# Conditioning tiles moved to another buffer ring, a further expert block taken into the loop, and a down projection placed inside the next block's gate and up

## The chip, the cores and the metric

The kernel runs on one core of one Trainium2 chip. The metric is device time in microseconds (us) of one execution. A core has five engines with a queue each: TensorE (PE, with its weight loads as PEld), VectorE (DVE), ScalarE (ACT), GpSimd (POOL) and SyncE (SP). In this kernel SP issues nearly all plain loads and stores, and POOL issues gathers, scatters and broadcasts. Sixteen DMA engines carry all of them.

## The reference

A backbone of two layers works on 512 tokens of width 1024, in float32. Layer 0 (even) has neighbourhood attention beside a short convolution, layer 1 (odd) has Hyena channels beside a conformer convolution. Each layer ends in a mixture of 16 experts with two experts per token. Shift, scale and gate of every part come from a conditioning vector:

```python
sh1, sc1, g1, sh2, sc2, g2 = split(silu(c) @ ada_w[l] + ada_b[l], 6)
u = rmsnorm(x, norm1_g[l]) * (1 + sc1) + sh1
y = odd_mixer(u, ...)                      # layer 1: w_in_odd, then long and short convolutions
x = x + g1 * (y @ w_out[l])
x = x + g2 * hier_moe(rmsnorm(x, norm2_g[l]) * (1 + sc2) + sh2, ...)
# hier_moe: act = silu(t @ w_gate) * (t @ w_up) * weight;  sum over experts of act @ w_down
```

The six conditioning vectors of a layer are three pairs: j=0 is (sh1, sc1), j=1 is (g1, sh2), j=2 is (sc2, g2). For layer 1, pair 0 is needed at the odd stage's start, pairs 1 and 2 only after it.

## The kernel before

**Split weights.** Every large product is made from three matmuls of rounded halves. A weight tile of 512 KB is loaded into a ring of five buffers called raw (L136). `split` (L141) lets ACT round it into a tile whi (L145), and DVE subtracts to make wlo (L146); whi and wlo each have four buffers. `mm3` issues the three matmuls (L159 to L161). A buffer is used again when all readers of its last content are done, so the SP load of a raw tile waits for the readers of the tile that lay there, and everything behind it in SP's queue waits too.

**The odd stage (about 587 to 845 us).** A string, ORDER (L65), sets the sequence of its pieces: v, p and x are projections of the three Hyena operands by column quarter, c the conformer's quarters, A and B the two long convolutions (as matrix products, L621 and L807), L a layer norm. Between the letters, tN takes N steps of a generator, `self.ada1` (L1111), that works pairs 1 and 2 of the conditioning through `ada_sums` (L230). For each pair it loads 16 tiles of ada_w, 512 KB each, into the same ring raw (`self.spare` is empty by then). DVE multiplies each tile by its column of silu(c) and adds it into adaacc (L246, L248). PE sums adaacc over the partitions (L254) into a PSUM bank, and `ada_done` adds the bias adab, which POOL has loaded at the generator's start (L235). For pair 2, `gain_rows` (L302) loads gainr through POOL (L305) and DVE multiplies it in (L307). The result goes to memory through SP (L268), and POOL reads it back spread over 128 partitions as gb (`bcast`, L323).

**After the odd stage** `mid` (L935) projects with w_out, adds the residual with the gate gb (L999, L1000), normalises with hm (L982), routes the tokens, and runs the expert blocks.

**Expert blocks.** Each expert takes up to 128 tokens as one block. POOL gathers the rows (L1307), PE turns them (L1318) and ACT and DVE split them into xt (L1321, L1324). `gate_up` (L1355) takes four weight tiles u=0 to 3: three are split, and the fourth goes unsplit through L1364 where the block is listed in FU. ACT and DVE make the activation (L1371, L1372), PE turns it (L1375), and L1378 and L1379 split it into at. `down` (L1383) takes two further tiles, and DVE scales the result into eo (L1396). POOL then adds it to memory by an indirect scatter (L1397); each scatter waits for the one before it. In the loop, the down of block b-1 is issued after the gate and up of block b (`late`).

**The further block.** If an expert has more than 128 tokens, the surplus makes a 17th block. In this run layer 1 has one such block and layer 0 none: there are 17 scatters to out and 16 to xd. The kernel before handles it in `extra_blocks` (L1117), under a run-time condition behind the whole loop: turn, six loads, gate and up, and down.

The order of instructions on each engine is set by a scheduler when the program is built, from the program order, buffers and dependencies.

## Time and profile before

| what | value |
|---|---|
| three runs of before | 1123.34, 1126.87, 1130.07 us (median 1126.87) |
| profiled execution | 1123.78 us |
| its span in the trace | 1121.7 us |
| mean granted TensorE clock | 0.944 |
| PE busy | 1023.0 us (91%) |
| DVE busy | 774.0 us (69%) |
| ACT busy | 497.9 us (44%) |
| POOL busy | 230.4 us (21%) |
| DMA | 240.78 MB, mean 215 GB/s |

The span is what the trace covers; the execution's own time is 2.1 us longer. Busy times are sums over instructions of one engine. A wait is idle time of an engine put down to whatever released it last, and the chain of waits follows the last instruction back through whatever released each step. Times in the rows are microseconds from the span's start.

### The profile page before, as it was taken

What the parts mean: (1) busy time and instruction counts of PE and PEld (TensorE: products, weight loads), DVE (VectorE), ACT (ScalarE), POOL (GpSimd) and SP (SyncE); (2) the same over time, 40 slices, a digit from 0 to 9 for tenths busy, and PEclk for the clock granted to TensorE, in tenths of its full rate; (3) what the DMA queues carried; (4) which work ended last, traced back from release to release, by engine and by line L of the source; (5) the groups of instructions that cost most, each with busy time, mean ns of one, the idle gap of its engine ahead of it and who ended that gap; (6) DMA issues with size and microseconds to landing.
All of it is one profiled execution on the core that took longest, in us unless ns stands there. A gap on an engine that the chain in (4) does not pass through costs nothing.

```text
span 1121.7 us, 14655 instructions
## 1 busy us (share of the span) xinstructions
PE 1023.0 (91%) x5118; PEld 755.2 (67%) x5118; DVE 774.0 (69%) x1255; ACT 497.9 (44%) x787; POOL 230.4 (21%) x244
## 2 busy tenths in 40 slices
PE   6999999999999599999987889899899859999994
PEld 2786787556787477777756667576477747777663
DVE  3462335587658798897967677757754577998883
ACT  3352223356434476577625323221253236766652
POOL 2031304011053223354221000000002121333311
PEclk8999999998999599999988899899989778999998
DMA  8825563686364479999825657634418786799893
GB/s 342 319 68 166 164 198 128 245 267 220 121 222 177 153 228 349 307 317 299 270 61 205 224 148 232 192 94 142 140 56 268 258 269 211 242 307 322 283 291 79
DMA packets 75374, 240.78 MB, mean 215 GB/s; under 512 B 15887, under 2 KB 17706, under 8 KB 75296
## 3 DMA queue, kind: packets, MB, share of 16 engines
q1 hardware_dynamic: 59840, 209.82, 55.0%
q0 software_dynamic: 15456, 29.98, 10.6%
q8 instruction: 42, 0.69, 0.3%
q14 instruction: 36, 0.29, 0.1%
HBM read 227.40 MB, written 25.72 MB: 226 GB/s over the span
## 4 chain that ended last, share of the span: by engine, by line
PE 65%; DMA 17%; DVE 8%; issue 5%; ACT 3%; POOL 1%; SPq 0%; POOLq 0%; DVEq 0%; ACTq 0%
PE mm L159 13%; PE mm L160 13%; PE mm L161 12%; DMA out<-eo,gi 6%; PE mm L225 3%; PE mm L1364 3%; PE sc L621 3%; PE mm L807 3%; DMA raw<-in_w_in_odd 2%; PE mm L580 2%; DVE wlo L146 2%; PE mm L621 2%; PE tr L1318 2%; DMA raw<-in_moe 2%; PE tr L569 2%
## 5 line engine op out<-in xcount | busy, mean ns | idle before, releaser
L146 DVE TENSOR_TENSOR wlo<-raw,whi 128x1024 fp32r<-128x1024 f32 x199 | 242.8, 1231 | 93.9 <-ACT whi L145 93.2
L145 ACT CAST whi<-raw 128x1024 fp32r<-128x1024 f32 x199 | 206.6, 1051 | 159.8 <-DMA raw<-in_w_in_odd 59.9
L159 PE MATMUL mm<-whi,xt 128*128 128x512 f32 x208 | 87.0, 418 | 2.4 <-ACT whi L145 2.4
L160 PE MATMUL mm<-wlo,xt 128*128 128x512 f32 x208 | 85.6, 412 | 3.3 <-DVE wlo L146 3.0
L161 PE MATMUL mm<-whi,xt 128*128 128x512 f32 x208 | 83.9, 403 | 0.0
L159 PE MATMUL mm<-u,whi 128*128 128x512 f32 x160 | 65.8, 414 | 5.9 <-ACT whi L145 5.3
L1307 POOL DMA_INDIRECT xe<-hd,gi x34 | 44.9, 1320 | 108.5 <-PE tr L1318 81.9
L161 PE MATMUL mm<-u,wlo 128*128 128x512 f32 x160 | 64.4, 404 | 0.3 <-DVE wlo L146 0.2
L160 PE MATMUL mm<-u,whi 128*128 128x512 f32 x160 | 64.4, 404 | 0.0
L1318 PE MATMUL tr<-ident,xe 128*128 128x128 f32 x264 | 41.6, 285 | 18.3 <-DMA xe<-hd,gi 16.0
L159 PE MATMUL mm<-whi,at 128*128 128x512 f32 x132 | 54.6, 448 | 1.0 <-ACT at L1378 0.9
L1396 DVE SCALAR_TENSOR_TENSOR eo<-mm,sw,gb 128x512 f32<-128x512 f32 x66 | 47.6, 744 | 10.6 <-PE mm L161 10.4
L160 PE MATMUL mm<-wlo,at 128*128 128x512 f32 x132 | 53.1, 417 | 0.0
L1397 POOL DMA_INDIRECT out<-eo,gi x17 | 33.2, 1953 | 96.1 <-DVE eo L1396 36.1
L1321 ACT CAST xt<-tr 128x512 fp32r<-128x512 f32 x66 | 32.4, 496 | 43.6 <-PE tr L1318 43.3
L161 PE MATMUL mm<-whi,at 128*128 128x512 f32 x132 | 51.0, 407 | 0.6 <-DVE at L1379 0.6
L1318 PEld LDWEIGHTS tr<-ident,xe 128*128 128x128 f32 x264 | 33.4, 148 | 26.3 <-issue 18.4
L160 PEld LDWEIGHTS mm<-wlo,xt 128*128 128x128 f32 x208 | 40.5, 195 | 14.7 <-DVE wlo L146 6.3
L159 PEld LDWEIGHTS mm<-whi,xt 128*128 128x128 f32 x208 | 40.3, 194 | 11.5 <-ACT whi L145 3.3
L1397 POOL DMA_INDIRECT xd<-eo,gi x16 | 33.3, 2079 | 71.7 <-DVE eo L1396 44.7
L1324 DVE TENSOR_TENSOR xt<-tr,xt 128x512 fp32r<-128x512 f32 x66 | 37.4, 570 | 14.8 <-ACT xt L1321 10.6
L743 POOL MEMSET pad<- 128x1 f32 x12 | 1.2, 100 | 225.5 <-DVE x L750 158.0
(402 smaller groups left out, 2439.0 us busy)
## 6 DMA issues: line engine op xcount, KB each, us to landing
raw<-in_moe SPq DMA_DIRECT2D x143, 512.0 KB
raw<-in_ada_w SPq DMA_DIRECT2D x64, 512.0 KB
mr<-in_moe SPq DMA_DIRECT2D x47, 512.0 KB
raw<-in_w_in_odd SPq DMA_DIRECT2D x20, 512.0 KB
bias<-in_ada_w SPq DMA_DIRECT2D x16, 512.0 KB
raw<-in_w_out SPq DMA_DIRECT2D x16, 512.0 KB
raw<-in_w_qkv SPq DMA_DIRECT2D x12, 512.0 KB
raw<-in_w_gch SPq DMA_DIRECT2D x12, 512.0 KB
```

Source lines behind the costliest of these rows:

```text
L145: nc.scalar.copy(hi, raw3)
L146: (lo_engine or nc.vector).tensor_tensor(lo, raw3, hi, op=ALU.subtract)
L159: nc.tensor.matmul(ps, lh, rh, start=first, stop=False)
L160: nc.tensor.matmul(ps, lh, rl, start=False, stop=False)
L161: nc.tensor.matmul(ps, ll, rh, start=False, stop=last)
L225: nc.tensor.matmul(ps[32 * g:32 * g + 32, :], self.cT[:, k, :], raws[g // 2][:, (g % 2) * 512:(g % 2) * 512 + 512], start=(k == 0), stop=( ...
L621: nc.tensor.matmul(ps[:, g * 256:g * 256 + 256], D[:, mat, :], s[:, r, :], start=(n == 0), stop=(n == 1))
L1307: self.fetched = self.nc.gpsimd.indirect_dma_start(out=xe, out_offset=None, in_=self.hd[l][:, :], in_offset=bass.IndirectOffsetOnAxis(ap=g ...
L1318: nc.tensor.transpose(pt[:, k * 128:k * 128 + 128], xe[:, (4 * h + k) * 128:(4 * h + k) * 128 + 128], self.ident)
L1324: nc.vector.tensor_tensor(xt[:, 1, 4 * h:4 * h + n, :].rearrange("p a b -> p (a b)"), pt[:, 0:n * 128], hi, op=ALU.subtract)
L1396: nc.vector.scalar_tensor_tensor(o[:, sl], ps, wt, g2b[:, sl], op0=ALU.mult, op1=ALU.mult)
L1397: nc.gpsimd.indirect_dma_start(out=self.dst[l][:, :], out_offset=bass.IndirectOffsetOnAxis(ap=di, axis=0), in_=o, in_offset=None, bounds_c ...
```

## The change

Three things are changed.

1. In `ada_sums`, the 32 ada_w tiles of layer 1's pairs 1 and 2 no longer go into ring raw. They take turns in the rings of whi and wlo, under the name adaw. The generator has two more stops per pair, ORDER takes two steps at c0, c2, c1 and c3 and none at A0 and B0 in exchange, and the bias load adab stands at the end of a pair and no longer at its start.
2. NXS says for each layer whether the further block is part of the loop. For layer 1 it is, without a condition: the loop has 17 blocks, SP reads the expert's number from xi (L1091 of the changed kernel), and the loads use the layer's usual rings. For layer 0 the condition stays.
3. In the last block of both layers, the down of the block before is issued between the second and third weight tile of gate and up (`mid=late`).

```diff
--- before.py
+++ after.py
@@ -32,7 +32,7 @@
 WA = [1, 1, 1, 0]
 CX = [2, 4]
 WE = [1, 0, 0, 0]
-XS = 1
+NXS = (0, 1)
 LF = 2
 RG = [2, 3, 4]
 KS = 4
@@ -58,11 +58,11 @@
 SB = 2
 QC = 0
 FE = 0
-FU = [[0, 1, 3, 4, 5, 6, 7, 8, 9, 10, 11, 12, 13, 14, 15], [1, 2, 3, 5, 6, 8, 9, 10, 11, 12, 13, 15]]
+FU = [[0, 1, 3, 4, 5, 6, 7, 8, 9, 10, 11, 12, 13, 14, 15], [1, 2, 3, 5, 6, 8, 9, 10, 11, 12, 13, 15, 16]]
 PM = 1
 PJ = 2
 PU = [[], []]
-ORDER = 'p1 t1 v1 t1 v0 t1 p0 t1 c0 t1 A0 t1 v3 t1 v2 t1 p2 t1 c2 t1 p3 t1 c1 t1 A1 x0 t1 c3 t1 x1 t1 B0 t1 x2 L0 x3 B1 t9'
+ORDER = 'p1 t1 v1 t1 v0 t1 p0 t1 c0 t2 A0 v3 t1 v2 t1 p2 t1 c2 t2 p3 t1 c1 t2 A1 x0 t1 c3 t2 x1 t1 B0 x2 L0 x3 B1 t9'
 TWO_PI = (6.28125, 0.0019350051879882812, float(2.0 * math.pi - 6.28125 - 0.0019350051879882812))
 P_, Q_ = (0, 1, 2, 3), (4, 5, 6, 7)
 NP1, NP2, NQ2, NQ3 = 8, 9, 10, 11
@@ -231,15 +231,14 @@
 
         nc, A = self.nc, self.A
         b = A["ada_b"]
-        bias = self.wk.tile([128, 512], F32, tag="t2", name="adab")
-        nc.gpsimd.dma_start(bias, bass.AP(tensor=b.tensor, offset=b.offset + l * 6144 + j * 2048,
-                                          ap=[[512, 4], [0, 32], [1, 512]]))
         for h in range(2):
             acc = self.ep2.tile([128, 1024], F32, tag="adaacc", name="adaacc", bufs=1)
             c0 = j * 2048 + h * 1024
             for k in range(8):
-                raw = self.spare.pop(0) if self.spare else self.rawp.tile([128, 1024], F32, tag="raw", name="raw")
-                if self.spare:
+                if l and j:
+                    raw = self.wp.tile([128, 1024], F32, tag=("whi", "wlo")[k % 2], name="adaw")
+                else:
+                    raw = self.spare.pop(0)
                     self.spare.append(raw)
                 nc.sync.dma_start(raw, A["ada_w"][l, k * 128:k * 128 + 128, c0:c0 + 1024])
                 if k == 0:
@@ -253,7 +252,13 @@
             for g in (2 * h, 2 * h + 1):
                 nc.tensor.matmul(ps[32 * g:32 * g + 32, :], self.onec.to_broadcast([128, 32]), acc[:, (g % 2) * 512:(g % 2) * 512 + 512],
                                  start=True, stop=True)
+            if not h:
+                yield
+        bias = self.wk.tile([128, 512], F32, tag="t2", name="adab")
+        nc.gpsimd.dma_start(bias, bass.AP(tensor=b.tensor, offset=b.offset + l * 6144 + j * 2048,
+                                          ap=[[512, 4], [0, 32], [1, 512]]))
         self.ada_done(l, j, ps, bias)
+        yield
 
     def ada_done(self, l, j, ps, bias):
         nc, A = self.nc, self.A
@@ -1077,19 +1082,23 @@
             xt = self.turn(rows[0], 0 in FU[l], m2)
             R["more"]()
             R["weights"]()
-        for b in range(16):
+        nb = 16 + NXS[l]
+        for b in range(nb):
             with self.tc.issue_after(self.routed.ins), self.tc.issue_after(self.last.ins):
                 self.tick(FILT[1] if b >= FB else FC)
-            load = self.ffn_weights(l, b, after=self.fetch0 if b >= EH[l] else None)
+            e = b
+            if b == 16:
+                e = nc.values_load(R["xi"][0:1, 1:2], engines=[mybir.EngineType.SP], min_val=0, max_val=15)
+            load = self.ffn_weights(l, e, after=self.fetch0 if b >= EH[l] else None, ring=b == 16)
             fetch(b + 1 + LA[l])
-            if b < 15:
+            if b < nb - 1:
                 nxt = self.turn(rows[b + 1], b + 1 in FU[l], m2)
             with self.tc.issue_after(self.routed.ins) if b == 0 else ExitStack(), self.tc.issue_after(self.lastT.ins):
-                part, xt = self.gate_up(m2, xt, load, b in FU[l], [i - 6 * b for i in PU[l]]), nxt
+                part, xt = self.gate_up(m2, xt, load, b in FU[l], [i - 6 * b for i in PU[l]], late if b == nb - 1 else None), nxt
             if b == 0:
                 with self.tc.issue_after(self.routed.ins):
                     self.extra_list(mp, R)
-            if late:
+            if late and b < nb - 1:
                 late()
             def late(a=(part, load, g2b, sel("gi", b), sel("wt", b), [i - 6 * b for i in PU[l]], [i - 2 * b for i in DE[l]])):
                 self.down(l, m2, *a)
@@ -1122,11 +1131,11 @@
 
         nc, nx, xi = self.nc, R["nx"], R["xi"]
         SP, DVE = mybir.EngineType.SP, mybir.EngineType.DVE
-        with self.tc.If(nx > 0):
-            if XS:
+        if not NXS[l]:
+            with self.tc.If(nx > 0):
                 xt = self.turn(xe, True, m2)
-            e = nc.values_load(xi[0:1, 1:2], engines=[SP], min_val=0, max_val=15)
-            self.ffn(l, m2, xt, g2b, R["gi"][:, 16:17], R["wt"][:, 16:17], e)
+                e = nc.values_load(xi[0:1, 1:2], engines=[SP], min_val=0, max_val=15)
+                self.ffn(l, m2, xt, g2b, R["gi"][:, 16:17], R["wt"][:, 16:17], e)
         with self.tc.If(nx > 1):
             with self.tc.For_i(1, nx, 1) as i:
                 e = nc.values_load(xi[0:1, bass.ds(i + 1, 1)], engines=[SP], min_val=0, max_val=15)
@@ -1325,11 +1334,11 @@
                                     op=ALU.subtract)
         return xt, xf
 
-    def ffn_weights(self, l, e, early=False, after=None):
+    def ffn_weights(self, l, e, early=False, after=None, ring=False):
 
         nc, A = self.nc, self.A
         src = A["moe"][l][e] if isinstance(e, int) else A["moe"][l][bass.ds(e, 1)].rearrange("o i p c -> (o i) p c")
-        where = "rrrrrr" if not isinstance(e, int) else PF[l][e] if e < len(PF[l]) else RING[l]
+        where = RING[l] if ring else "rrrrrr" if not isinstance(e, int) else PF[l][e] if e < len(PF[l]) else RING[l]
         for i in range(6):
             if where[i] == "b" and not early:
                 yield self.early[l, e, i]
@@ -1352,12 +1361,14 @@
         load = self.ffn_weights(l, e)
         return self.down(l, m2, self.gate_up(m2, xt, load, True), load, g2b, di, wt)
 
-    def gate_up(self, m2, xt, load, full, pool=()):
+    def gate_up(self, m2, xt, load, full, pool=(), mid=None):
 
         nc = self.nc
         xt, xf = xt
         ps = self.mmt()
         for u in range(4):
+            if u == 2 and mid:
+                mid()
             raw = next(load).rearrange("p (k c) -> p k c", k=2)
             if full and u == 3:
                 for k in range(2):
```

**SP at the start of the odd stage**, behind the loads xr of the layer's input. raw and adaw are the loaded tiles, in_w_in_odd the odd stage's projection weights, and in_ada_w the conditioning weights. Before:

```order
L136 DMA raw_5655<-in_w_in_odd 128x1024
L244 DMA raw_5697<-in_ada_w 128x1024
L244 DMA raw_5700<-in_ada_w 128x1024
L136 DMA raw_5703<-in_w_in_odd 128x1024
L244 DMA raw_5742<-in_ada_w 128x1024
L244 DMA raw_5745<-in_ada_w 128x1024
L136 DMA raw_5748<-in_w_in_odd 128x1024
L244 DMA raw_5787<-in_ada_w 128x1024
L244 DMA raw_5790<-in_ada_w 128x1024
L136 DMA raw_5793<-in_w_in_odd 128x1024
L244 DMA raw_5832<-in_ada_w 128x1024
```

After the change:

```order
L136 DMA raw_5655<-in_w_in_odd 128x1024
L136 DMA raw_5701<-in_w_in_odd 128x1024
L136 DMA raw_5746<-in_w_in_odd 128x1024
L136 DMA raw_5791<-in_w_in_odd 128x1024
L136 DMA raw_5837<-in_w_in_odd 128x1024
L243 DMA adaw_5695<-in_ada_w 128x1024
L243 DMA adaw_5698<-in_ada_w 128x1024
L243 DMA adaw_5740<-in_ada_w 128x1024
L243 DMA adaw_5743<-in_ada_w 128x1024
L136 DMA raw_5869<-in_w_in_odd 128x1024
L136 DMA raw_5901<-in_cfx 128x1024
```

Projection loads and conditioning loads alternated in one ring; now five projection loads stand in front, and the conditioning loads have buffers of other rings.

**POOL behind the odd stage**, from the layer norm's lnr on. gb is the gate read back from memory, gainr the norm gain, wr and cst the router's constants. Before:

```order
L192 TENSOR_TENSOR lnr_6961<-lnr_6959,mhalf_94 128x4
L323 DMA gb_7141<-ada11_79 128x1024 x2
L305 DMA gainr_7119<-in_norm2_g 64x1x512
L953 DMA wr_7147<-in_wr 128x160
L955 DMA cst_7149<-in_br 128x20
```

After the change:

```order
L192 TENSOR_TENSOR lnr_6953<-lnr_6951,mhalf_94 128x4
L328 DMA gb_7141<-ada11_79 128x1024 x2
L258 DMA adab_7115<-in_ada_b 128x1x512
L310 DMA gainr_7119<-in_norm2_g 64x1x512
L958 DMA wr_7147<-in_wr 128x160
```

The bias load of pair 2 now stands between the gate's two reads and the load of gainr; before, it was issued during the odd stage (row of L235 at 689.0 us in the trace). On DVE the addition `adar<-mm,adab` moved with it, to directly ahead of `adar<-adar,gainr`.

**DVE at the end of layer 1's experts.** xt are the split token rows, wlo a split weight tile, act and at the activation, eo the scaled result (L1324, L146, L1372, L1379 and L1396 before; L1333, L146, L1383, L1390 and L1407 after). Before:

```order
L1396 SCALAR_TENSOR_TENSOR eo_9416<-mm_9417,sw_7663,gb_7144 128x512
L1396 SCALAR_TENSOR_TENSOR eo_9416<-mm_9425,sw_7663,gb_7144 128x512
L1293 TENSOR_LOAD xi_7848
L1125 COMPARE_AND_BRANCH
L1324 TENSOR_TENSOR xt_9437<-tr_9439,xt_9437 128x512
L1324 TENSOR_TENSOR xt_9437<-tr_9446,xt_9437 128x256
L146 TENSOR_TENSOR wlo_9468<-raw_9465,whi_9467 128x1024
L146 TENSOR_TENSOR wlo_9480<-raw_9477,whi_9479 128x1024
L146 TENSOR_TENSOR wlo_9492<-raw_9489,whi_9491 128x1024
L146 TENSOR_TENSOR wlo_9517<-raw_9514,whi_9516 128x1024
L146 TENSOR_TENSOR wlo_9523<-raw_9520,whi_9522 128x1024
L1372 TENSOR_TENSOR act_9505<-act_9505,mm_9464 128x256
```

After the change:

```order
L146 TENSOR_TENSOR wlo_9459<-raw_9456,whi_9458 128x1024
L146 TENSOR_TENSOR wlo_9465<-raw_9462,whi_9464 128x1024
L1390 TENSOR_TENSOR at_9386<-tr_9383,at_9386 128x256
L146 TENSOR_TENSOR wlo_9491<-raw_9488,whi_9490 128x1024
L1407 SCALAR_TENSOR_TENSOR eo_9468<-mm_9469,sw_7663,gb_7144 128x512
L146 TENSOR_TENSOR wlo_9516<-raw_9513,whi_9515 128x1024
L1407 SCALAR_TENSOR_TENSOR eo_9468<-mm_9477,sw_7663,gb_7144 128x512
L146 TENSOR_TENSOR wlo_9522<-raw_9519,whi_9521 128x1024
L1383 TENSOR_TENSOR act_9504<-act_9504,mm_9431 128x256
L1390 TENSOR_TENSOR at_9510<-tr_9507,at_9510 128x256
L1407 SCALAR_TENSOR_TENSOR eo_9525<-mm_9526,sw_7663,gb_7144 128x512
L1407 SCALAR_TENSOR_TENSOR eo_9525<-mm_9534,sw_7663,gb_7144 128x512
```

The further block's work stood in a row of its own behind the 16th block's last eo (eo_9416); now its five wlo stand around the 16th block's two eo (eo_9468), and the branch is gone.

## Rows read from the trace of the kernel before

**Rows 1.** The page, busy time of the engines and the chain that ended last, whole span.

```profile
PE 1023.0 (91%) x5118; PEld 755.2 (67%) x5118; DVE 774.0 (69%) x1255; ACT 497.9 (44%) x787; POOL 230.4 (21%) x244
...
PE 65%; DMA 17%; DVE 8%; issue 5%; ACT 3%; POOL 1%; SPq 0%; POOLq 0%; DVEq 0%; ACTq 0%
```

**Rows 2.** Windows in the odd stage: us, PE, PEld, DVE, ACT, POOL busy, clock, DMA, GB/s.

```profile
600.00:840.00 240.00, 220.54 (x1098) 155.81 (x1099) 173.55 (x197) 69.03 (x95) 5.28 (x30) 0.94 0.49 151
...
620.00:630.00 10.00, 4.97 (x14) 3.25 (x13) 5.52 (x6) 2.87 (x4) 0.00 (x0) 0.72 0.82 238
...
700.00:710.00 10.00, 4.88 (x13) 3.77 (x14) 6.01 (x6) 2.97 (x5) 0.00 (x0) 0.66 0.77 220
...
790.00:800.00 10.00, 7.97 (x27) 5.68 (x27) 6.26 (x9) 2.57 (x5) 0.00 (x0) 0.83 0.59 165
```

**Rows 3.** Waits in 587 to 845 us: engine line, releaser, total, times, longest.

```profile
ACT whi L145 <- DMA raw<-in_w_in_odd: 59.9, 13, 10.6
```

**Rows 4.** The chain of waits through the odd stage: start us, us, what.

```profile
615.21 1.20 DVE adaacc L248
616.43 8.96 DMA raw<-in_w_in_odd
625.41 1.05 ACT whi L145
...
695.06 8.13 DMA raw<-in_w_in_odd
...
712.12 3.46 PE sc L621 x16
...
772.06 3.44 DMA raw<-in_w_in_odd
```

**Rows 5.** The timeline at the second stall: start us, us, engine, instruction, idle before.

```profile
704.80 1.12 PE L760 MATMUL tr<-ident,x 128*128 128x128 f32 x4 [5.19 <-ACT ur L761]
...
706.23 5.46 PE L621 MATMUL sc<-ur,D 128*128 128x256 f32 x16 [0.32 <-ACT ur L761]
```

**Rows 6.** The page, one of the costliest groups (count, busy, mean ns, idle before).

```profile
L146 DVE TENSOR_TENSOR wlo<-raw,whi 128x1024 fp32r<-128x1024 f32 x199 | 242.8, 1231 | 93.9 <-ACT whi L145 93.2
```

**Rows 7.** The chain at the end of layer 0's experts.

```profile
570.12 1.42 DVE eo L1396 x2
...
571.81 6.31 DMA xd<-eo,gi
...
578.85 6.50 DMA xd<-eo,gi
```

**Rows 8.** POOL's timeline there: start us, us, engine, instruction, idle before.

```profile
562.39 2.41 POOL L1397 DMA_INDIRECT xd<-eo,gi  x1 [7.31 <-DVE eo L1396]
```

**Rows 9.** The chain after the odd stage.

```profile
845.04 12.12 DMA gainr<-in_norm_g
...
868.33 0.69 DVE hm L982
```

**Rows 10.** A window of 10 us behind that chain.

```profile
870.00:880.00 10.00, 7.89 (x27) 5.87 (x28) 6.95 (x8) 4.40 (x8) 2.18 (x1) 0.66 1.02 394
```

**Rows 11.** The timeline of layer 1's end, DVE, ACT and PE.

```profile
1095.36 0.75 DVE L1396 SCALAR_TENSOR_TENSOR eo<-mm,sw,gb 128x512 f32<-128x512 f32 x1 [0.18 <-PE mm L161]
...
1096.80 3.90 ACT L145 CAST whi<-raw 128x1024 fp32r<-128x1024 f32 x4
...
1106.72 0.38 ACT L1371 ACTIVATE act<-mm 128x256 f32<-128x256 f32 x1 [2.59 <-PE mm L1364]
...
1111.62 0.75 DVE L1396 SCALAR_TENSOR_TENSOR eo<-mm,sw,gb 128x512 f32<-128x512 f32 x1 [0.18 <-PE mm L161]
```

**Rows 12.** The chain of layer 1's scatters.

```profile
1093.08 6.92 DMA out<-eo,gi
...
1100.76 6.86 DMA out<-eo,gi
...
1112.65 1.55 POOL out L1397
```

## Prediction

> **What bounds the kernel now.** I read the page first. PE is busy for 1023.0 of 1121.7 us, DVE for 774.0, and of the chain that ended last 65% is PE and 17% DMA [rows 1]. So most of the time is matmul, and what a change of order can win lies where PE stands still or runs slow. The windows show where that is in the odd stage: over 600 to 840 us PE is busy for 220.54 of 240 us, so 19.5 us are idle, and three windows of 10 us hold most of it, with 4.97, 4.88 and 7.97 us busy and granted clocks of 0.72, 0.66 and 0.83 [rows 2]. The waits then name the releaser: ACT's rounding whi waits 59.9 us in 13 waits for projection loads, 10.6 us the longest [rows 3]. Most of that is covered, since PE still has split tiles to work on; it is uncovered in the three windows.
>
> The chain tells why these loads come late. At 615.21 DVE multiplies a conditioning tile (adaacc). Only when it ends is its raw buffer free, and only then, at 616.43, does SP issue the next projection load; it takes 8.96 us, and whi starts at 625.41. The same happens at 695.06 (8.13 us) and, shorter, at 772.06 (3.44 us) [rows 4]. So a projection tile, needed at once, waits in one ring behind a conditioning tile that nothing needs before 845 us. The second stall also shows the clock: PE is idle for 5.19 us behind a small ACT copy that stands behind the late whi, and its next 16 matmuls take 5.46 us [rows 5], where 16 of the same line take 3.46 us at 712.12 [rows 4].
>
> **The odd stage's ring (part 1 of the change).** Added and removed work is nil: 32 loads, 32 DVE multiplies and four PE sums per pair stay. What moves is who waits. The projection loads now have ring raw to themselves, five stand first in SP's queue, and their buffers come free when the wlo of an earlier tile is done.
>
> - First stall: 10 less 4.97 is 5.0 us idle. A mean clock of 0.72 means that 56% of the window, 5.6 us, was granted half speed (1.2 instead of 2.4 GHz), which costs from nothing (all of it in the idle time) to 2.8 us; I take 1.5. Sum 6.5.
> - Second: 5.19 idle and 5.46 less 3.46 for the slow matmuls, 7.2.
> - Third: 10 less 7.97 is 2.0 idle; 0.83 means 3.4 us at half speed, up to 1.7 lost; I take 1. Sum 3.
>
> Together 16.7, taken as 17 us. The most that could go: the three windows hold 12.2 of the 19.5 us idle; all of these, half of the other 7.3 (whose releasers are several), and 2.8, 2.0 and 1.7 for the clock make 22.3. The least is nothing, and less than nothing is the last rival.
>
> A page of the Trainium skill says the time of matmuls should not be read by busy share: "Perfetto Trace Analysis", section Identifying the Most-Contended Engine, holds that matmul busy time is a poor measure of the headroom. The trace agrees with it here, for the 16 matmuls count as busy at 5.46 us as they do at 3.46. By busy share alone the three stalls would give 12.2 us, and the whole sum would be 4.5 us smaller.
>
> What is late next is the new wait. A conditioning tile now holds a buffer of whi or wlo, four each, and two steps apart the split that wants that buffer waits for the tile's load and its multiply. The load takes 3.44 to 8.96 us by the rows of loads [rows 4], the multiply 1.2, so a tile stays for 5 to 10 us. The stage's 240 us hold 16 pairs of tiles, 15 us for each pair, and a buffer returns after four allocations, about two such times. So I cost it at nothing.
>
> **The bias load (also part 1).** adab of pair 2 is 256 KB and stood in the middle of the odd stage. It now stands on POOL between the two reads of gb and gainr. Queued behind it are gainr, DVE's multiply, the store of the pair, its reading back, and hm. In the trace gainr lands 12.12 us after its issue at 845.04, and hm starts at 868.33 [rows 9]. Behind it PE is uncovered: 7.89 us busy at a clock of 0.66 [rows 10], so what is added here is added to the end. The 12.12 us carry the 1024 KB of gb and the 128 KB of gainr; 256 KB at that rate are 2.7 us, and one more DVE addition of about 0.69 us (hm's row) stands in the chain. Bounds: 0, if the bias lands beside the others, and 3.4. I take 3, by the rate's row.
>
> By "DMA: Bandwidth & Descriptors" of the Trainium skill, section Queues, rings and completion order, each DMA engine takes the queues in turn, packet by packet, so POOL's queue would get an even share beside SP's. At half of the 394 GB/s of the later window that would be an estimate of 1.3 us, and the sum would be 1.4 lower; no run here shows the packets in turn, and the 12.12 us speak for a smaller share.
>
> **Layer 0's last block (part 3).** In the chain, block 14's eo ends at 571.5 and its scatter runs from 571.81 for 6.31, then block 15's from 578.85 for 6.50; the next layer's loads wait for that one [rows 7]. Block 14's down now comes ahead of the second half of block 15's gate and up. The scatter before began at 562.39 [rows 8]; at 6.4 us and 0.6 of gap, block 14's could begin at 569.4 instead of 571.81, so 2.4 us are the most. Block 15's own eo must then be earlier too, which its later half does not promise, so 0 is the least; I take the middle, 1.2.
>
> **Layer 1's end (parts 2 and 3).** Block 15's eo ends at 1096.1. The further block then runs alone: four roundings in 3.90 us from 1096.80, the activation at 1106.72, its last eo at 1111.62 [rows 11], 16.3 us behind block 15's. In the loop its turn, splits and matmuls lie beside block 15's. What then binds is the chain of scatters: 1093.08 and 6.92, 1100.76 and 6.86, so the last could begin at 1107.6 and 0.7, 1108.3, instead of 1112.65 [rows 12]: at most 4.4 us earlier. Block 15's down now comes behind half of the further block's gate and up, but its scatter had to wait until 1100.76 anyhow, 4.7 us behind its eo; that is the cover, and if it does not do, the gain shrinks by as much. I take 4, least 0. SP reads xi once more ahead of later expert loads; the nearest row is the gap of 0.76 us between two scatters, where POOL reads it, so 0 to 0.8, and I take 0, since 17 loaded tiles of other buffers lie ahead. The work of the further block is the same, because this layer does have one.
>
> **Sum.** 17 and 1.2 and 4 gained, 3 lost: 19.2 us. Against the profiled execution's 1123.8 us (span 1121.7) that is 1104.6; this execution is 3.1 us below the median of the three runs, 1126.87, and against the median the sum gives 1107.7, which I forecast.
>
> **Rivals.**
>
> *The odd stage gives most of it back.* SP is still one queue in order. Where a conditioning load waits for a whi buffer that PE has not left, the projection load behind it waits as before, only for PE instead of DVE. For it: in the changed order conditioning loads still stand ahead of projection loads after the first five. Against it: the five prefetched tiles. If only 5 of the 17 us remain, the sum is 7.2 and the time 1119.7. Chance 0.13.
>
> *The end gains nothing, and only the ring pays.* Block 15's scatter may begin late, for its down now stands behind more splits on DVE (1.23 us each [rows 6]). With neither end paying the sum is 14 and the time 1112.9. Chance 0.14.
>
> *Slower, through the split buffers.* If a conditioning tile stays longer than those two step times, some 30 us, or if DVE comes to its multiply late because it stands behind a wlo whose tile has not landed, each of the 16 pairs holds back a split by a multiply and a subtraction, 1.2 and 1.23 us [rows 4, 6], together 2.4. Sixteen times that is 39 us, and with the other terms the time is 1126.9 less 19.2 and 39, 1147. It decides from 1.2 us per pair on, where the whole gain is gone. For it: DVE is in order and busy for 173.55 of 240 us [rows 2]. Against it: a stay of 5 to 10 us. Chance 0.08.
>
> **How the numbers follow.** The forecast has the remaining 0.65. About 0.5%, 5.6 us, is what a measurement of this kernel can tell from no change, so faster means below 1121.2. The forecast and the second rival lie below it (0.79); the first lies at it, and I give half of it to each side; the slower rival counts as slower but for 0.01. So faster 0.85, same 0.08, slower 0.07. Best bounds (22.3, 2.4, 4.4 and no bias) sum to 29.1, so 1098; the first rival with 2 us more is 1122. Those are the range.
>
> **What would show it.** Right: ACT's wait for projection loads falls from 59.9 us to below 20, the three windows are filled at full clock, the odd stage ends 15 to 19 us earlier, gainr lands about 3 us later behind gb, and the last scatter follows the one before it within 1 us. Wrong: whi waits for PE or DVE in the odd stage (a split buffer), SP's queue stands at adaw, or PE's idle time comes back among the experts, where the DMAs or the scatters would then be what binds.

## The result and the profile after

The changed kernel takes 1111.32 us in the median of four runs (1110.59 to 1112.4), before took 1126.39 us beside it (1123.34 to 1130.07). The ratio is 0.9871, its 95% interval 0.9834 to 0.9908: 15 us faster, where 19.2 had been forecast, and inside the range of 1098 to 1122. The profiled execution took 1110.59 us, its span is 1108.8 us, 12.9 less than the span of before. The page, busy time of the engines:

```profile
PE 1017.9 (92%) x5118; PEld 749.5 (68%) x5118; DVE 774.1 (70%) x1255; ACT 497.9 (45%) x787; POOL 233.7 (21%) x244
```

The instructions are as many as in [rows 1]. PE's busy time is 5.1 us lower for the same 5118 instructions, DVE's is the same, so some 8 of the 12.9 us are idle time of PE. The table follows the gain along the two profiled executions. Each row is a stretch between two events that both traces have.

| stretch | before | after | gained | forecast |
|---|---|---|---|---|
| start to the 13th scatter to xd (identical work) | 547.24 | 545.08 | 2.16 | none |
| to the last scatter to xd (layer 0's end) | 31.61 | 30.95 | 0.66 | 1.2 |
| loads of layer 1's input (585.37; 582.50) to the gate's read gb (843.86; 830.45) | 258.49 | 247.95 | 10.5 | 17 |
| gb to the first hm (867.72; 857.33) | 23.86 | 26.88 | -3.0 | -3 |
| hm to the last scatter (1112.65; 1099.50) | 244.93 | 242.17 | 2.8 | 4 |

The first row is no effect of the change: PE, DVE, ACT and POOL run the same instructions in the same order up to there, and the traces of the experiments below reach that scatter between 543.9 us (e11) and 547.9 us (e12; e9, which has a smaller ring, is left out). So of the 12.9 us of span about 11 are the change's.

**The odd stage**, in five pieces that hold the same work in both kernels, but for up to four matmuls at each cut. Columns: us, busy us (x instructions) of PE, PEld, DVE, ACT and POOL, granted clock, DMA share, GB/s. Before:

```profile
585.40:600.00 14.60, 8.50 (x36) 6.13 (x34) 7.55 (x18) 8.12 (x21) 2.51 (x4) 0.85 0.92 338
600.00:640.00 40.00, 34.91 (x145) 27.57 (x146) 30.26 (x35) 15.01 (x19) 2.08 (x10) 0.87 0.63 199
640.00:700.00 60.00, 56.48 (x297) 42.12 (x295) 45.73 (x51) 17.83 (x25) 1.65 (x11) 1.00 0.59 176
700.00:790.00 90.00, 83.70 (x432) 55.55 (x432) 63.96 (x71) 20.11 (x28) 0.26 (x4) 0.96 0.49 147
790.00:843.90 53.90, 49.36 (x243) 33.80 (x244) 35.04 (x46) 19.98 (x29) 1.33 (x6) 0.91 0.30 95
sum 258.50, PE 232.94 PEld 165.17 DVE 182.54 ACT 81.05 POOL 7.83; mean PE 46.59 PEld 33.03 DVE 36.51 ACT 16.21 POOL 1.57
```

After the change:

```profile
582.50:597.00 14.50, 11.59 (x40) 8.14 (x38) 7.96 (x18) 9.42 (x22) 2.51 (x4) 0.74 0.95 367
597.00:636.00 39.00, 35.14 (x145) 28.13 (x146) 30.62 (x34) 13.39 (x18) 1.37 (x9) 0.87 0.63 226
636.00:696.00 60.00, 56.71 (x297) 40.39 (x296) 43.90 (x50) 19.75 (x28) 1.40 (x11) 1.00 0.53 164
696.00:778.00 82.00, 80.31 (x428) 53.52 (x426) 64.60 (x71) 19.41 (x29) 0.25 (x4) 1.00 0.53 165
778.00:830.40 52.40, 48.76 (x246) 32.97 (x247) 35.59 (x45) 17.97 (x26) 1.29 (x5) 0.93 0.25 76
sum 247.90, PE 232.51 PEld 163.16 DVE 182.67 ACT 79.95 POOL 6.82; mean PE 46.50 PEld 32.63 DVE 36.53 ACT 15.99 POOL 1.36
```

PE's busy time is 232.94 and 232.51 us, so over the whole stage nearly all of the 10.5 us are idle time: 25.6 before, 15.4 now. The fourth piece is 8 us shorter (90 and 82). Its idle time fell by 4.6 us and its busy time by 3.4, with four matmuls fewer and a granted clock of 1.00 instead of 0.96. It holds the second stall of [rows 2]; the third lies across its end at 790 us. The first two pieces together, with the first stall, gave 1.1 us. The stalls are better told apart between events of PE that both traces have:

| stretch of the odd stage | before | after | gained | forecast |
|---|---|---|---|---|
| loads of the input to the transposition of v ahead of the second stall (698.57; 694.40) | 113.20 | 111.90 | 1.3 | 6.5, first stall |
| to the third product sc<-Di,T (782.18; 770.61) | 83.61 | 76.21 | 7.4 | 7.2, second stall |
| to the next matmuls of wide (798.97; 785.54) | 16.79 | 14.93 | 1.9 | 3, third stall |
| to the gate's read gb | 44.89 | 44.91 | 0.0 | none |

Three further traces below have the same ring and the same late bias load: e1, e5 (the changed kernel again) and e7. Against the same trace of before they gained 3.2, 1.7 and 1.5 us in the first row, 7.4 in the second in all three, and 0.0, -0.1 and 2.4 in the third. A second trace with the old ring (e2) has 113.4, 83.0 and 19.3 us there. So the second row is firm, while the others differ among traces of one ring by as much as they gained.

Which waits of PE those were, by the view of waits (engine line, releaser, total, times, longest). Before, 600 to 840 us:

```profile
PE mm L159 <- ACT whi L145: 5.3, 2, 5.0
PE tr L760 <- ACT ur L761: 5.2, 1, 5.2
PE sc L621 <- ACT b L624: 3.2, 1, 3.2
```

After, 597 to 827 us:

```profile
PE mm L253 <- DVE adaacc L247: 2.8, 1, 2.8
PE mm L161 <- DVE wlo L146: 2.5, 2, 2.1
...
PE tr L351 <- DVE u L359: 1.6, 1, 1.6
```

The three entries of before, 13.7 us, are gone from the list; in their place stand two waits that hang on the conditioning tiles, 2.8 and 2.5 us, and one on the stage's input. The wait of 2.8 us is the third stall under another name: it lies in the same product, between its 8th and 9th matmul. Before (PE), and after (PE, then ACT):

```profile
792.03 7.00 PE L621 MATMUL sc<-ur,D 128*128 128x256 f32 x24 [3.22 <-ACT b L624]
```

```profile
779.13 1.05 PE L253 MATMUL mm<-adaacc,onec 128*32 128x512 f32 x4 [2.80 <-DVE adaacc L247]
780.11 5.50 PE L626 MATMUL sc<-ur,D 128*128 128x256 f32 x24
```

```profile
775.86 1.04 ACT L145 CAST whi<-raw 128x1024 fp32r<-128x1024 f32 x1 [4.22 <-DMA adaw<-in_ada_w]
...
777.96 0.56 ACT L629 COPY b<-sc 128x512 f32<-128x512 f32 x1
```

PE's sum of adaacc stood ahead of this product before (785.84) and now stands inside it, and it waits for the last multiply, which ends at 779.07. The copy b, which PE waited for before, would have held it until 778.52 anyhow, again behind a late whi, and that whi now waits for the landing of a conditioning tile.

ACT's own waits changed their releaser [rows 3]:

```profile
ACT whi L145 <- DVE adaacc L247: 28.8, 4, 11.7
...
ACT whi L145 <- PE mm L160: 19.7, 7, 4.6
```

No load of a projection weight holds ACT any more in this trace. A multiply (adaacc) holds it instead, 28.8 us in four waits, because the split tile's buffer lies behind a conditioning tile. How that comes about at the stage's start is seen on three engines. DVE, in order:

```profile
610.54 0.76 DVE L245 TENSOR_SCALAR adaacc<-adaw,cT 128x1024 f32<-128x1024 f32 x1
...
611.81 1.28 DVE L247 SCALAR_TENSOR_TENSOR adaacc<-adaw,cT,adaacc 128x1024 f32<-128x1024 f32 x1
...
613.73 1.28 DVE L247 SCALAR_TENSOR_TENSOR adaacc<-adaw,cT,adaacc 128x1024 f32<-128x1024 f32 x1
614.92 1.22 DVE L146 TENSOR_TENSOR wlo<-raw,whi 128x1024 fp32r<-128x1024 f32 x1
...
618.79 1.28 DVE L247 SCALAR_TENSOR_TENSOR adaacc<-adaw,cT,adaacc 128x1024 f32<-128x1024 f32 x1 [0.86 <-DMA adaw<-in_ada_w]
```

SP at the same time, and then ACT:

```profile
597.60 0.33 SPq L136 DMA_DIRECT2D raw<-in_cfx  x1
615.03 0.33 SPq L243 DMA_DIRECT2D adaw<-in_ada_w  x1
```

```profile
620.11 1.05 ACT L145 CAST whi<-raw 128x1024 fp32r<-128x1024 f32 x1 [7.73 <-DVE adaacc L247]
```

The first four conditioning tiles were issued at 587 to 592 us, but DVE does not multiply one before 610.54, since in its order the stage's input comes first. The third multiply ends at 615.01, and only then is a buffer free for the fifth tile, whose load SP has held until 615.03 (13.6 us in SP's waits), with everything behind it. That tile's multiply begins at 618.79, and the whi that needs its buffer at 620.11; PE has other tiles by then and waits 0.38 us for the wlo that follows. The wlo at 614.92 stands behind three multiplies; PE waits 2.12 us for it.

**Behind the odd stage**, POOL and DVE (columns: start us, us, engine, instruction, idle before it and its releaser):

```profile
830.45 1.16 POOL L328 DMA_DIRECT2D gb<-ada  x2 [8.76 <-PE mm L161]
832.28 0.72 POOL L258 DMA_DIRECT2D adab<-in_ada_b  x1 [0.67 <-DVE yc L894]
833.00 0.70 POOL L310 DMA_DIRECT2D gainr<-in_norm_g  x1
```

```profile
844.33 0.69 DVE L266 TENSOR_TENSOR adar<-mm,adab 128x512 f32<-128x512 f32 x1 [6.05 <-DMA adab<-in_ada_b]
846.61 0.68 DVE L312 SCALAR_TENSOR_TENSOR adar<-adar,gainr 64x512 f32<-64x512 f32 x1 [1.58 <-DMA gainr<-in_norm_g]
...
857.33 1.29 DVE L987 TENSOR_TENSOR hm<-xr,gb 128x512 f32<-128x512 f32 x2 [4.51 <-DMA gb<-ada]
```

The bias load adab stands between gb and gainr. DVE waits 6.05 us for it. From gb to the gain's multiply it is 16.16 us (830.45 to 846.61); before it was 13.32 (843.86 to 857.18), where gainr alone was waited for [rows 9].

**Layer 0's end** (POOL) and **layer 1's end** (POOL, and the chain of waits there):

```profile
568.28 1.78 POOL L1408 DMA_INDIRECT xd<-eo,gi  x1 [6.78 <-DVE eo L1407]
...
576.03 1.58 POOL L1408 DMA_INDIRECT xd<-eo,gi  x1 [2.57 <-DVE eo L1407]
```

```profile
1092.74 1.55 POOL L1408 DMA_INDIRECT out<-eo,gi  x1 [6.04 <-DVE wlo L146]
1099.50 1.55 POOL L1408 DMA_INDIRECT out<-eo,gi  x1 [5.21 <-DMA out<-eo,gi]
```

```profile
1092.74 6.01 DMA out<-eo,gi
```

The last scatter begins 6.76 us behind the one before it, 0.75 us after that one's end (1092.74 and 6.01); before, 11.89 us lay between them [rows 12].

### The profile page after: what moved, and what is told of

It reads as the page before. It is cut to its first block, busy times and chain, and to the rows that moved or that the text cites. A ratio compares the mean times of both kernels' runs of the same rounds, so it can differ in the third digit from the quotient of the medians.

```text
span 1108.8 us, 14652 instructions
## 1 busy us (share of the span) xinstructions
PE 1017.9 (92%) x5118; PEld 749.5 (68%) x5118; DVE 774.1 (70%) x1255; ACT 497.9 (45%) x787; POOL 233.7 (21%) x244
## 5 line engine op out<-in xcount | busy, mean ns | idle before, releaser
L146 DVE TENSOR_TENSOR wlo<-raw,whi 128x1024 fp32r<-128x1024 f32 x199 | 242.8, 1232 | 72.4 <-ACT whi L145 71.4
L159 PE MATMUL mm<-whi,xt 128*128 128x512 f32 x208 | 85.4, 411 | 0.4 <-ACT whi L145 0.4
L161 PE MATMUL mm<-whi,xt 128*128 128x512 f32 x208 | 82.5, 396 | 0.1
L1407 DVE SCALAR_TENSOR_TENSOR eo<-mm,sw,gb 128x512 f32<-128x512 f32 x66 | 47.8, 745 | 10.1 <-PE mm L161 9.6
L1408 POOL DMA_INDIRECT xd<-eo,gi x16 | 36.4, 2277 | 67.8 <-DVE eo L1407 47.3
L1333 DVE TENSOR_TENSOR xt<-tr,xt 128x512 fp32r<-128x512 f32 x66 | 37.5, 570 | 14.7 <-ACT xt L1330 11.2
```

The costliest lines, as they stand in the source:

```text
L146: (lo_engine or nc.vector).tensor_tensor(lo, raw3, hi, op=ALU.subtract)
L159: nc.tensor.matmul(ps, lh, rh, start=first, stop=False)
L161: nc.tensor.matmul(ps, ll, rh, start=False, stop=last)
L1333: nc.vector.tensor_tensor(xt[:, 1, 4 * h:4 * h + n, :].rearrange("p a b -> p (a b)"), pt[:, 0:n * 128], hi, op=ALU.subtract)
L1407: nc.vector.scalar_tensor_tensor(o[:, sl], ps, wt, g2b[:, sl], op0=ALU.mult, op1=ALU.mult)
L1408: nc.gpsimd.indirect_dma_start(out=self.dst[l][:, :], out_offset=bass.IndirectOffsetOnAxis(ap=di, axis=0), in_=o, in_offset=None, bounds_c ...
```

## The experiments

The theory after the two traces: the parts add up (ring 10.5, bias -3, ends 3 to 5), and the missing 6 us of the ring's 17 are the first stall, which the split rings have kept. Twelve runs followed, one of them (e5) the changed kernel again. "Stage" is from the loads of the odd stage's input on SP to the read of gb on POOL: 258.5 us before, 248.0 after.

**The parts alone.** e1 is part 1 without the others:

```diff
-NXS = (0, 1)
+NXS = (0, 0)
-... late if b == nb - 1 else None), nxt
+...), nxt
-            if late and b < nb - 1:
+            if late:
```

> Part 1 alone: conditioning tiles in the rings of the split weights, new ORDER, bias load at the pair's end; the further block is back under its condition and the down of the block before stands behind the last block's gate and up. Theory: the parts add up, and the changed kernel's trace gives 10.5 us gained in the odd stage, 2.9 lost in the bias chain and 4.6 gained by the last scatter, so this one is 7 to 9 us faster than before (ratio 0.992 to 0.994), with the last scatter 16 us behind the 16th block's as before. Rival: the ring gives nothing that lasts and the ends pay for all: within 2 us of before.

e2 has parts 2 and 3, with `ada_sums` and ORDER as before:

```diff
...
-                if l and j:
-                    raw = self.wp.tile([128, 1024], F32, tag=("whi", "wlo")[k % 2], name="adaw")
-                else:
-                    raw = self.spare.pop(0)
+                raw = self.spare.pop(0) if self.spare else self.rawp.tile([128, 1024], F32, tag="raw", name="raw")
...
```

> Parts 2 and 3 alone: further block in the loop, down inside the last gate and up; conditioning tiles, ORDER and bias load as before. Theory: 4 to 5.5 us faster than before (ratio 0.995 to 0.9965), the last scatter starting within 0.6 us of the end of the one before it. Rival: the ends only pay when the experts start earlier, and the scatter chain takes it back here: 0 to 1.5 us.

e1: 1113.56 us, ratio 0.9899 (0.9867 to 0.9931). e2: 1119.29 us, ratio 0.9952 (0.9927 to 0.9977). Against before's median of 1124.42 us these are 10.9 and 5.1 us; together 16, against 15 for the whole change in its first runs and 12.4 in e5 below. The stage of e1 is 247.9 us (582.80 to 830.71), that of e2, with the old ring, 262.3 (582.12 to 844.40), which is 3.8 us longer than in the trace of before. The last two scatters on POOL, in e1 and in e2:

```profile
1091.83 2.39 POOL L1408 DMA_INDIRECT out<-eo,gi  x1 [7.35 <-DVE wlo L146]
1102.80 1.55 POOL L1408 DMA_INDIRECT out<-eo,gi  x1 [8.59 <-DVEq L1139]
```

```profile
1101.34 1.55 POOL L1403 DMA_INDIRECT out<-eo,gi  x1 [7.05 <-DMA out<-eo,gi]
1108.10 1.55 POOL L1403 DMA_INDIRECT out<-eo,gi  x1 [5.21 <-DMA out<-eo,gi]
```

The ends are worth about 5 us by themselves and the ring, with its late bias, 11; each is clear of the noise, and neither rival holds. That they add up is not shown: the ratio of e1 alone, 0.9899, is that of the whole change in e5. e1 gave somewhat more than the 7 to 9 expected, and in e2 the last scatter began 0.76 us behind the end of the one before, where 0.6 was expected.

**The bias load.** e3, the changed kernel with the load at the pair's start:

```diff
+        bias = self.wk.tile([128, 512], F32, tag="t2", name="adab")
+        nc.gpsimd.dma_start(bias, ...)
         for h in range(2):
...
-        bias = self.wk.tile([128, 512], F32, tag="t2", name="adab")
-        nc.gpsimd.dma_start(bias, ...)
         self.ada_done(l, j, ps, bias)
```

> The changed kernel with the bias load back at the start of each pair. Theory: the chain behind the odd stage is 2.5 to 3 us shorter (gainr lands about 12 us behind its issue and needs no addition ahead of it), and since PE is uncovered there the time is 2 to 3 us below the changed kernel, 1108.5. Rival: the bias tile held through the odd stage takes one of four small buffers from the convolutions and costs as much as it saves: within 1 us of 1111.

1108.31 us (ratio 0.9841, 0.9792 to 0.9889), 3 below the changed kernel, but not in the same runs; so both were run again, together:

> The changed kernel once more, beside the next three on one chip. Theory and rival alike: within 1 us of its first median of 1111.3, ratio to before 0.986 to 0.990, and a profile with the same lead at the odd stage's end (10 to 11 us counted from the loads of the layer's input).

> The bias load back at each pair's start, again, now beside the changed kernel. Theory: 2 to 3 us below it, as the chain from the gate's read to the norm gain's multiply is 2.5 us shorter and PE is uncovered behind it. Rival: the first run's profile had given 1.2 of it back in the odd stage and showed the first scatter at the same time as the changed kernel, so 0 to 1 us.

The changed kernel took 1110.83 us (ratio 0.9899, 0.9868 to 0.9930), 12.4 less than before's median of 1123.19, the one with the early bias 1110.14 (0.9898, 0.9868 to 0.9928). e5's stage is 249.6 us (583.11 to 832.66), a lead of 8.9 us and not the 10 to 11 expected: at the third stall PE waits 3.31 us in it, and the 24 matmuls take 6.67 us. The gain's multiply in e3:

```profile
845.38 0.68 DVE L312 SCALAR_TENSOR_TENSOR adar<-adar,gainr 64x512 f32<-64x512 f32 x1 [4.47 <-DMA gainr<-in_norm_g]
```

From gb (831.89) to it are 13.49 us, 13.24 in e6, against 16.16 and 14.55 (832.66 to 847.21) in the two traces of the changed kernel. So between these traces the late bias costs 1.3 to 2.9 us in its chain, and over all kept traces less clearly (14.55 to 16.16 us in five with the late load and whole conditioning, 12.85 to 14.84 in six with the early one and the usual rings). The time shows at most a part of it: 0.7 us between medians that each spread by 5. That e6's theory of 2 to 3 us fell is what the runs say; where the rest is given back was not found.

**The steps' places.** e4 takes the first two steps out at p1 and v1 and puts them behind B0:

```diff
-ORDER = 'p1 t1 v1 t1 v0 t1 p0 t1 c0 t2 ... x1 t1 B0 x2 L0 x3 B1 t9'
+ORDER = 'p1 v1 v0 t1 p0 t1 c0 t2 ... x1 t1 B0 t2 x2 L0 x3 B1 t9'
```

> The changed kernel with the first two steps of the generator taken out at p1 and v1 and put behind B0. Theory: the first stall did not go because the first conditioning tiles hold split buffers until DVE, busy with the stage's input, comes to their multiplies at 610 to 620 us; with the steps two letters later whi of the first projections no longer waits for a multiply, PE is idle 2 to 5 us less between 600 and 640, and the time is 2 to 5 us below the changed kernel. Rival: the wait only moves to the letters where the steps are then, or to the PSUM sum at the end: within 1 us of 1111, or slower.

1122.35 us (1117.29 to 1129.4), ratio 0.9988 (0.9954 to 1.0021): 11 us above the changed kernel, and the stage is 264.7 us (581.95 to 846.63). PE's waits in the stage:

```profile
PE tr L765 <- issue: 6.8, 1, 6.8
PE sc L626 <- DVE zt L856: 6.0, 2, 5.4
PE mm L812 <- DMA wide<-sg: 5.4, 1, 5.4
```

And DVE ahead of the longest of them, a transposition of v that PE starts at 642.97 (the view names no releaser for it, but v ends at 642.87):

```profile
638.79 1.28 DVE L247 SCALAR_TENSOR_TENSOR adaacc<-adaw,cT,adaacc 128x1024 f32<-128x1024 f32 x1
...
641.78 1.09 DVE L755 SCALAR_TENSOR_TENSOR v<-pad,hsw,sc 128x512 f32<-128x512 f32 x1
```

The waits for wlo went, as the theory had it, from 2.5 us to 0.4. But the stretch up to the second stall is not shorter, 115.1 us against 111.9, for v now stands on DVE behind the multiplies that come two letters later, and so do zt and what the first convolution loads. The rival holds: the wait moves to the letters where the steps are. The other way round, e12 keeps the ring and the early bias and takes the step places of before:

```diff
-... p0 t1 c0 t2 A0 v3 t1 ... c2 t2 p3 t1 c1 t2 A1 x0 t1 c3 t2 x1 t1 B0 x2 ...
+... p0 t1 c0 t1 A0 t1 v3 t1 ... c2 t1 p3 t1 c1 t1 A1 x0 t1 c3 t1 x1 t1 B0 t1 x2 ...
```

> The changed kernel with the bias load first and the ORDER string of before (one step at c0, A0, c2, c1, c3 and B0 each, instead of two at the c's): the ring alone, without the new places of the steps. Theory: the ring makes the gain, and a step moved by one letter does little: stage 247 to 251 us, time 1108 to 1112, ratio to before 0.985 to 0.990. Rival: the steps' places matter as much as the ring, as two steps moved from p1 and v1 to B0 cost 11 us: stage over 254 us and time over 1114.

1111.96 us (1103.05 to 1115.97), ratio 0.9888 (0.9833 to 0.9942), stage 252.0 us (585.01 to 837.04). The stage is between the two theories, 1 us over the first; the time is the first one's. The ring makes the gain, and the new places of the steps are worth 0.7 to 2.8 us of the stage beside the other kernels with the early bias (249.2 in e3, 251.4 in e6), which is hardly more than these two traces of one kernel differ.

**Part 3 alone taken out.** e7 is the changed kernel with e1's two edits on `late`, NXS as changed:

> The changed kernel without part 3: the further block is in the loop, the down of the block before stands behind the whole gate and up of the last block, in both layers. Theory: the gain at the end comes from the loop (turn, loads and splits beside the 16th block), and the placement of the down only matters for layer 0's 0.65 us; within 1.5 us of the changed kernel, and the last scatter still within 1 us of the end of the one before. Rival: without the down in the middle the last scatters bunch up, 2 to 4 us slower.

1109.42 us (1105.44 to 1112.88), ratio 0.9893 (0.9853 to 0.9933), and its last scatter begins 6.92 us behind the one before (1087.56, 1094.48). In layer 0, from the 13th scatter to the last, it takes 31.47 us, e1 without the piece 31.60, the change 30.95. So placing the down inside gate and up is worth 0.5 to 0.65 us at layer 0's end and nothing that can be seen at layer 1's; there the loop alone brings the gain.

**What the tiles still cost.** e8 cuts the multiplies to 64 columns, all but the first of each eight, in the kernel with the early bias:

```diff
-                    nc.vector.scalar_tensor_tensor(acc, raw, self.cT[:, k, 0:1], acc, ...)
+                    nc.vector.scalar_tensor_tensor(acc[:, 0:n], raw[:, 0:n], self.cT[:, k, 0:1], acc[:, 0:n], ...)
```

> The kernel of the last but one run, with the multiplies of the conditioning tiles cut to 64 of 1024 columns (all but the first of eight; this leaves most of the conditioning of pairs 1 and 2 out, so only the odd stage is to be read). Theory: DVE's multiplies, each 1.28 us in its queue, are what still holds back the split buffers: ACT's waits for them fall from some 30 us to under 12 and the odd stage, from the loads of its input to the gate's read, is 3 to 7 us shorter than with whole multiplies. Rival: the tiles' loads, not the multiplies, hold the buffers: waits and stage within 2 us.

The stage is not shorter but longer, 259.8 us (583.46 to 843.27). ACT's waits for the multiplies, and DVE's for the tiles:

```profile
ACT whi L145 <- DVE adaacc L251: 24.7, 5, 10.6
DVE adaacc L251 <- DMA adaw<-in_ada_w: 23.5, 8, 6.2
```

24.7 us are over the 12 that the theory allowed, and the stage is 10.6 us longer than e3's 249.2, so neither theory nor rival holds. In this order it is not the multiply's length that holds the buffer: DVE stands 23.5 us with the multiply at its head and the tile not landed (5.5 us in the changed kernel). A shorter instruction also changes the order that the scheduler writes, so this is no clean subtraction. The whole time of this kernel, 1139.26 us, and of e10 below, 1154.68, is not compared: with other conditioning the router chooses otherwise, and at the end one further block of an expert runs in e8 and two in e10, with one and two scatters by a further list of indices (gix) from 1113 us on.

e9 gives the tiles one buffer of their own (and ring raw four):

```diff
-                    raw = self.wp.tile([128, 1024], F32, tag=("whi", "wlo")[k % 2], name="adaw")
+                    raw = self.ep2.tile([128, 1024], F32, tag="adaw", name="adaw", bufs=1)
```

> The changed kernel with the bias load first, the 32 conditioning tiles in one buffer of their own, and ring raw cut from five buffers to four to make room (which also touches the experts, so the odd stage is what is read). Theory: what is left of the stall is that a split buffer stands behind a conditioning tile, so here ACT's waits for the multiplies (28 to 35 us in the changed kernel) are zero by construction and the stage, from the loads of its input to the gate's read, is 248 us in the changed kernel and 241 to 246 here. Rival: SP's single queue and DVE's order are the limit, one buffer makes SP wait for each multiply, and the stage takes 250 us or more.

1154.27 us, stage 283.5 us (588.45 to 871.93). ACT waits for no multiply, but DVE does for the tiles:

```profile
DVE adaacc L250 <- DMA adaw<-in_ada_w: 46.3, 20, 6.4
```

46.3 us in 20 waits: each load is issued only after the multiply before it, and splits stand behind the waiting multiply. The rival holds; sharing the split rings is better than one private buffer. How much of the 35 us more the smaller ring raw costs was not separated.

e10 leaves 24 of the 32 tiles out:

```diff
-            for k in range(8):
+            for k in (0, 1) if l and j else range(8):
```

> The changed kernel with the bias load first and 8 of the 32 conditioning tiles; the other 24 loads and multiplies are left out, and with them three quarters of the conditioning of pairs 1 and 2, so only the odd stage is read. It shows how much the tiles still cost in the stage. Theory: the stage is 6 to 9 us shorter than the 248 us of the changed kernel, which is about what the prediction's 17 us had promised and the measured 10.5 did not give. Rival: within 3 us; then the tiles no longer cost anything and the 17 us were wrong for another reason.

The stage is 249.9 us (584.65 to 834.50). Its sum over five pieces, and PE's longest wait:

```profile
sum 249.80, PE 232.23 PEld 164.42 DVE 155.52 ACT 79.67 POOL 8.12; mean PE 46.45 PEld 32.88 DVE 31.10 ACT 15.93 POOL 1.62
```

```profile
PE sc L626 <- ACT ur L766: 4.6, 1, 4.6
```

With a quarter of the tiles DVE is 27 us less busy, PE's busy time is the same 232.2 us, and the stage is no shorter than the 248.0 of the changed kernel. The rival's number came, but this is no clean subtraction either. The generator now ends a pair after four steps and not ten, so the tiles come earlier: the last multiply is at 663.26 us, where it is at 777.79 in the changed kernel. The third stall is indeed gone, 11.6 us in its stretch against 14.9 and, before, 16.8; in exchange the stretch up to the second stall takes 115.8 us against 111.9, with the wait of 4.6 us above in it. So where the tiles are they still cost something, and that the stage would be as long without any is not shown. What is left idle, 17.6 us here and 15.4 in the changed kernel, is at the input, at small ACT copies and at the convolutions' loads.

**The best pieces together.** e11 has the ring, the loop, the early bias, and no down in the middle (e3 and e7 together):

> Conditioning tiles in the split rings, further block in the loop, but the bias load at each pair's start and no down inside the last gate and up: the pieces that looked best by themselves. Theory: 1 to 4 us below the changed kernel's 1111, 1107 to 1110, ratio to before 0.984 to 0.988. Rival: the pieces overlap, as PE is busy nearly all the time among the experts: 1110 to 1112.

1111.06 us (1103.46 to 1112.16), ratio 0.9878 (0.9852 to 0.9904). The rival holds; no version was found that is faster than the changed kernel beyond the noise.

## Why the prediction was right, and what was mis-sized

Right were the sign, the second stall, the place of the bias in its chain, and the chain of scatters at the end of layer 1. The time came nearer to the forecast than its parts did: the parts that the traces show sum to 11 us of the 19.2, and that the first medians differ by 15 is partly luck (12.4 in e5). By its steps:

- **Second stall.** Forecast 7.2, measured 7.4 in all four traces. Its idle time of 5.19 us is 0.24, and the 16 matmuls behind it take 3.71 us instead of 5.46 [rows 5].
- **First stall: the step that was mis-sized most.** "So I cost it at nothing", of the conditioning tile in a split ring. The prediction compared a tile's stay, 5 to 10 us, with two step times, 30 us. But a tile does not leave when it has landed and DVE is idle: the first of the four early ones was multiplied 23 us after its issue (587.19 to 610.54), behind the stage's input in DVE's order, the fifth was loaded only after that, and whi stood behind it until 620.11. Of the 6.5 us 1.3 came (1.5 to 3.2 in the other traces). In the second piece the idle time is 3.9 us where it was 5.1: 2.5 us of waits for wlo that hang on the tiles and 1.6 for the stage's input have come in place of the 5.0. Its busy time and clock are as before (0.87), so the 1.5 us for the clock did not come either. It was nearly the second condition of the slower rival (DVE late because of its order), at two places and not at sixteen. That the tiles are all of it is argued from these waits and not shown: neither e4 nor e10 made the stretch shorter. That the places of the steps matter was shown by e4 (11 us slower).
- **Third stall: the same step.** Forecast 3, measured 1.9 in this pair. PE's wait itself is hardly shorter, 2.5 to 3.3 us in four traces against 3.2 and 3.9 in the two with the old ring, as a conditioning tile holds whi there, and through it the copy b, and the sum of adaacc stands in the product besides. The window of 790 to 800 us had shown only 2.0 of the 3.2 us.
- **The signs.** Of the signs of being wrong two came true: whi waits for DVE and PE (28.8 and 19.7 us), and SP stands at adaw, in the stage 27.8 us behind multiplies and 26.2 behind PE. So the mechanism of the first rival is there too, but most of these waits are covered on PE. Of the signs of being right, ACT's wait for projection loads is gone, gainr lands 2.8 us later behind gb, and the last scatter follows within 1 us; the stage's end came 10.5 us earlier and not 15 to 19.
- **The clock's part.** The sum took 4.5 us for matmuls at half clock. At the second stall 1.75 of its 2.0 us came back. At the third, 1.5 came in the changed kernel (24 matmuls in 7.00 and 5.50 us) and little or nothing in e5 and e1 (6.67 and 7.18). PE's busy time over the stage fell by 0.4 us only (232.94 to 232.51), since the first piece has 3.1 us more of it, with four more matmuls and a granted clock of 0.74 instead of 0.85. The page "Perfetto Trace Analysis" of the Trainium skill (section Identifying the Most-Contended Engine) had been weighed there: its rule that matmul busy time is a poor measure of the headroom is borne out by those 16 matmuls, though the page's reason for it is that matmuls are pipelined, and here it is the clock. The sum by busy share alone, 4.5 us smaller, 14.7, was nearer to the 15 us measured, but by luck: it gives the second stall 5.2 us, where 7.4 came, and the first 5.0, where 1.3 came.
- **The bias.** Forecast 3, measured 3.0 from gb to hm in the changed kernel, 1.5 in its second trace (832.66 to 857.98, 25.32 us). The estimate of 1.3 us by "DMA: Bandwidth & Descriptors" (section Queues, rings and completion order), with POOL's queue at an even share, would fit the second trace and not the first; no run shows the packets in turn. The prediction's "1.4 lower" holds for the bias term: as it is a loss, the whole gain would have been 1.4 us larger, 20.6.
- **Layer 0's end.** Forecast 1.2, measured 0.66 here and 0.5 to 0.65 against kernels without the piece.
- **Layer 1's end.** Forecast 4, measured 2.8 between hm and the last scatter here and 5 in e2 alone. That the scatters would bind was right: 0.75 us lie between the end of one and the start of the last. That the down in the middle takes part in it was not: e7.
- **The rivals.** "Gives most back" (1119.7) did not come, "the end gains nothing" neither (e2: 5 us).

What stays open: how much of the first stall the tiles cost, why the late bias's 1.3 to 2.9 us do not show in the medians, and what makes the expert part of one and the same kernel 5 us longer or shorter (below).

## What to carry to other kernels

A load that nobody needs soon should not share a ring with one that is needed at once, but moving it to another ring only helps where that ring's readers come to it early: ask when its consumer gets to it in its own order, not how long load and operation take. When stalls are summed, ask for each one what the engine would wait for next at the same place: the second stall here had nothing behind it and gave all that was forecast, and at the third the moved tiles' own sum and a split behind another tile took the place of what went. A block that runs alone behind a loop is worth its serial latency less the chain that then binds, here 5 of 16 us.

## What the runs showed of the chip that was not expected

The same program varies in two places. Up to the first scatter to xd all kernels but e9 run the same instructions in the same order, and their traces reach it between 409.06 us (e11) and 412.68 (e10). And the part from the first hm to the last scatter took 242.95 us in e3 (856.45 to 1099.40) and 237.98 in e6 (858.79 to 1096.77), which are the same kernel; 4.5 of these 5 us lie ahead of the first scatter to out (91.39 and 86.94 us from hm). The six runs of e11 lie at 1103.5 to 1103.8 (two) and 1110.8 to 1112.2 (four). A difference of 2 or 3 us between two single traces of this kernel therefore says little. The ring's gain in the stage does not rest on one pair: the stage took 258.5 and 262.3 us with the old ring (before, e2) and 247.3 to 252.0 in the eight traces with the new one, whole conditioning and the first two steps in place.
